# Attention scores of an encoder layer: from two 128-row products a head to three 64-row products a head, two heads in the two halves of the array

## Chip, cores and metric

The kernel runs on one core of one Trainium2 chip. The metric is the device time of one execution in microseconds; the time before is the median of three runs. TensorE does the matrix products. The profile calls its products PE and its loads of the stationary operand PEld. VectorE is DVE, ScalarE is ACT, GpSimd is POOL, and SyncE, whose queue issues nearly all transfers here, is SP.

## The reference, cut to what matters

One layer: RMSNorm, one wide input projection, two token mixers beside each other (chunked band attention with 8 heads of 64, and an mLSTM with 4 heads of 128), gates, an output projection, a feed-forward network with squared ReLU, a final RMSNorm. 2048 tokens, 1024 features, float32. The change lies in the band attention:

```
def chunk_band_attention(q, k, v, rel_bias):        # q, k, v: (1, 2048, 8, 64)
    # chunks of 64 tokens; a chunk sees itself and the 8 chunks before it
    scores = einsum('bclhd,bckhd->bchlk', qc, kband) * (1 / sqrt(64))
    scores = scores + bias                          # per head, by clipped distance
    scores = where(valid, scores, -1e30)
    p = softmax(scores, axis=-1)
    out = einsum('bchlk,bckhd->bclhd', p, vband)
```

## The kernel before

**Products in float32 from split operands.** Every float32 operand of a large product is held as two parts, a high part rounded to the matrix format (fp32r) and a low part that is the rest. ACT writes the high part, DVE subtracts it. The large products then take three matrix products, high by high, high by low and low by high (`mm3`, L488 to L490).

**Blocks.** The 2048 tokens are four blocks of 512. Blocks 0 and 1 ("near") are projected with plain tiles in `dense`. Blocks 2 and 3 ("far") are projected, together with the feed-forward network, by schemes of seven products of quarter matrices (`quad`, `quad_tok`, `down`; the products of L571 and L599), and their q and k come back from HBM: `parts` stores a high and a low part of each pair of heads to `qfar` and `kfar`. The attention of blocks 2 and 3 runs beside `down` of the first half.

**The order of the work** is set by a planner written in the kernel (`Flow`). Each piece of work is a generator that yields what it needs: `("pe", ns)`, `("act", ns)`, `("dve", ns)`, `("sp", ns, latency)` for a time on an engine, `"get"` for buffers of a pool, `"wait"` for events. The planner keeps a clock for each engine and gives the engine to the thread that can start first; the large products (priority 5) fill what is left. The order so found is the order in which each engine's queue is written, and each engine then executes its queue in order.

**Pools that the attention uses.** `rpool` has 28 tiles of 128 x 2 x 512, `bias` 2 of 128 x 640, `sc` 4 pairs of a score tile (128 x 640) and its statistics (128 x 4), `temp` 6 of 128 x 516, `banks` the 8 PSUM banks of 128 x 512.

**The attention of one block, per head h of pair j = h / 2:**

- Layout. A head's k tile has the high part of k in rows 0 to 63 and the low part in rows 64 to 127; column part 0 holds the block before, part 1 its own block. A head's q tile has the high part of q in both halves of the rows (part 0), and the low part in both (part 1). So one product over 128 rows adds q_high by k_high and q_high by k_low, and a second one adds q_low by both parts of k.
- Near blocks: `evac_q` (L1094) takes a bank of the projection, in which rows 0 to 63 are one head and rows 64 to 127 the other, and for each head writes the high part twice on ACT (L1101, L1103), the low part on DVE (L1105), and copies it on DVE (L1108). `evac_k` (L1113) writes high on ACT (L1120) and low on DVE (L1122). `spill_k` (L1128) stores k for the next block, and `head` (L1133) loads that of the block before.
- Far blocks: `head_far` (L1037) loads both parts of k and q of the head from HBM, q twice, for the two halves of the rows.
- `head_rest` (L1141) gets one bias tile, loads the head's bias (L1147), blocks out two corners on POOL (L1149, L1150), and starts two `unit`s, each for two query tiles of 128 tokens. The bias tile goes back at the end of both units.
- `unit` (L1170) gets two `sc` and starts `scores` for each of its tiles; when both are soft, it starts `turn` for groups of up to four 128 x 128 transposes (L1286, split by L1289 on ACT and L1291 on DVE), and `weigh`, the product with v (L1220).
- `scores` (L1244): a tile has 640 columns of keys (fewer in block 0), in two halves if it has over 256. Each half is two products (L1255) into a bank; DVE adds the bias and finds the extreme (L1261); then the exponential with its sum on ACT (L1270), the reciprocal (L1272) and the scaling on DVE (L1274).
- The end of `weigh`: v's two parts give two halves of the bank's rows; ACT copies one half (L1230), DVE adds the other (L1232), and the head's 64 rows are split into the mixer tile `mix[j]` by ACT (L1237) and DVE (L1239).

A block's scores go in groups of four products (two halves, two products each). A far block's attention has product groups of the scores, of the transposes and of `weigh` between products of `mm3`.

A place outside the attention that the prediction reads: `gates` (L1310) multiplies over 40 rows, so its stationary operand and its moving one lie in rows 0 to 39. It runs four times, once a block.

Of the kernel before, what the change touches and what calls it, by code (L numbers as in the profile page):

```python
# [29 lines left out]
P = 128  # L30
# [185 lines left out]
def dve_ns(n):  # L216
    return 70 + 1.042 * n
# [7 lines left out]
class Layer:  # L225
# [8 lines left out]
    def make_tiles(self, pool, psum):  # L234
# [36 lines left out]
        self.rec_room = Pool([0] * N_REC)  # L271
# [702 lines left out]
    def attention(self, b):  # L974
# [8 lines left out]
        for j in range(4):  # L983
# [9 lines left out]
            for i in range(2):  # L993
                h = 2 * j + i
                k, q = yield "get", self.rpool, 2
                B["kq"][h] = (k, q)
                fl.set(B["kq_ev"][h])
                fl.spawn(self.head(b, h), 1)
# [7 lines left out]
    def attention_far(self, b):  # L1006
# [7 lines left out]
        for j in range(4):  # L1014
# [12 lines left out]
            for i in range(2):  # L1027
                h = 2 * j + i
                k, q = yield "get", self.rpool, 2
                B["kq"][h] = (k, q)  # L1030
                fl.spawn(self.head_far(b, h), 1)
# [4 lines left out]
    def head_far(self, b, h):  # L1036
        fl, nc, B = self.fl, self.nc, self.blk[b]  # L1037
        k, q = B["kq"][h]
        j, rows = h // 2, slice(h % 2 * 64, h % 2 * 64 + 64)
        kf = k.bitcast(F32)  # L1040
        for n, x in ((0, b - 1), (1, b)):
            if x < 2:
                yield "wait", [self.blk[x]["k_spilt"][h]]
                yield "sp", 900, 2000
                nc.sync.dma_start(kf[:, n], self.kdram[x].ap().bitcast(F32)[h])
            else:
                yield "wait", [self.k_ev[x, j]]
                yield "sp", 900, 2000
                for a in range(2):
                    nc.sync.dma_start(kf[a * 64:a * 64 + 64, n], self.kfar[x].ap()[j, a, rows])  # L1050
        yield "wait", [self.q_ev[b, j]]
        yield "sp", 900, 2000
        for a in range(2):
            nc.sync.dma_start(q.bitcast(F32)[a * 64:a * 64 + 64],
                              self.qfar[b].ap()[j, :, rows].rearrange("a p c -> p a c"))
        fl.set(B["q_ev"][h])
        fl.set(B["k_ev"][h])
        yield from self.head_rest(b, h, k, q)
# [35 lines left out]
    def evac_q(self, b, j, bk):  # L1094
        fl, nc, B = self.fl, self.nc, self.blk[b]
        yield "wait", [B["kq_ev"][2 * j], B["kq_ev"][2 * j + 1]]
        for i in range(2):
            q = B["kq"][2 * j + i][1]
            src = bk[i * 64:i * 64 + 64]
            yield "act", act_ns(512, True)  # L1100
            nc.scalar.mul(q[0:64, 0], src, 0.125)  # L1101
            yield "act", act_ns(512, True)
            nc.scalar.mul(q[64:128, 0], src, 0.125)  # L1103
            yield "dve", dve_ns(512)
            nc.vector.scalar_tensor_tensor(q[0:64, 1], src, 0.125, q[0:64, 0].bitcast(F32),  # L1105
                                           op0=ALU.mult, op1=ALU.subtract)
            yield "dve", dve2_ns(512)
            nc.vector.tensor_copy(q[64:128, 1], q[0:64, 1].bitcast(F32))  # L1108
            fl.set(B["q_ev"][2 * j + i])
        fl.put_dense(self.banks, bk)  # L1110

    def evac_k(self, b, j, bk):
        fl, nc, B = self.fl, self.nc, self.blk[b]  # L1113
        yield "wait", [B["kq_ev"][2 * j], B["kq_ev"][2 * j + 1]]
        for i in range(2):
            h = 2 * j + i
            k = B["kq"][h][0]
            src = bk[i * 64:i * 64 + 64]
            yield "act", act_ns(512, True)
            nc.scalar.copy(k[0:64, 1], src)  # L1120
            yield "dve", dve_ns(512)
            nc.vector.tensor_sub(k[64:128, 1], src, k[0:64, 1].bitcast(F32))  # L1122
            fl.set(B["k_ev"][h])
            if b + 1 < NB:
                fl.spawn(self.spill_k(b, h, k), 2)
        fl.put_dense(self.banks, bk)

    def spill_k(self, b, h, k):  # L1128
        yield "sp", 900, 2000
        self.nc.sync.dma_start(self.kdram[b].ap().bitcast(F32)[h], k[:, 1].bitcast(F32))  # L1130
        self.fl.set(self.blk[b]["k_spilt"][h])

    def head(self, b, h):  # L1133
        fl, nc, B = self.fl, self.nc, self.blk[b]
        k, q = B["kq"][h]
        if b > 0:
            yield "wait", [self.blk[b - 1]["k_spilt"][h]]
            yield "sp", 900, 2000
            nc.sync.dma_start(k[:, 0].bitcast(F32), self.kdram[b - 1].ap().bitcast(F32)[h])
        yield from self.head_rest(b, h, k, q)  # L1140

    def head_rest(self, b, h, k, q):
        fl, nc, B = self.fl, self.nc, self.blk[b]
        (bias,) = yield "get", self.bias, 1
        yield "sp", 1500, 2000
        rb = self.io["rb"]
        nc.sync.dma_start(bias, bass.AP(rb.tensor, h * 768, [[1, P], [1, 640]]))  # L1147
        yield "pool", 180
        nc.gpsimd.memset(bias[0:64, 0:64], NEG)  # L1149
        nc.gpsimd.memset(bias[64:128, 576:640], NEG)  # L1150
        yield "wait", [B["q_ev"][h], B["k_ev"][h]]
# [1306 lines left out]
```

## Time and profile before

| | before |
|---|---|
| time, median of 3 runs | 2865.05 us (2863.65 to 2865.47) |
| profiled execution: span, first to last instruction | 2865.0 us |
| mean granted TensorE clock | 0.994 |
| PE busy | 2815.4 us, 98% |
| PEld busy | 2350.6 us, 82% |
| DVE busy | 2037.9 us, 71% |
| ACT busy | 1558.1 us, 54% |
| moved to and from HBM | 605.74 MB in packets, mean 211 GB/s |

The profiled execution's own time is its span, 2865.0 us; it lies between the lowest and the highest of the runs.

How to read it: "busy" is the union of an engine's instruction times. Products are pipelined, so the duration given for one product is longer than the time that it adds to a stream; the distance between the starts of two neighbours shows that. A group's row gives the line, the engine, the operation, the tiles and their shapes, the count, the busy time and the mean of one, then the idle time of the engine in front of these instructions and what ended it. In a timeline row the first number is the start and the second the length of the merged stretch, both in us. For matrix products "128*40" is rows by columns of the stationary operand.

### The profile page before, as it was taken

What the parts mean: (1) busy time and instruction counts of PE and PEld (TensorE: products, weight loads), DVE (VectorE), ACT (ScalarE), POOL (GpSimd) and SP (SyncE); (2) the same over time, 40 slices, a digit from 0 to 9 for tenths busy, and PEclk for the clock granted to TensorE, in tenths of its full rate; (3) what the DMA queues carried; (4) which work ended last, traced back from release to release, by engine and by line L of the source; (5) the groups of instructions that cost most, each with busy time, mean ns of one, the idle gap of its engine ahead of it and who ended that gap; (6) DMA issues with size and microseconds to landing.
All of it is one profiled execution on the core that took longest, in us unless ns stands there. A gap on an engine that the chain in (4) does not pass through costs nothing.

```text
span 2865.0 us, 39043 instructions
## 1 busy us (share of the span) xinstructions
PE 2815.4 (98%) x13576; PEld 2350.6 (82%) x13576; DVE 2037.9 (71%) x3783; ACT 1558.1 (54%) x2701; POOL 48.2 (2%) x116
## 2 busy tenths in 40 slices
PE   8999999999999999999999999999999999999998
PEld 7888888888878888877888888788778788888887
DVE  6886479778896867875666887778876744455565
ACT  4664366755444545664556666446644655554444
POOL 0000000000000000000000000000000000000000
PEclk9999999999999999999999999999999999999999
DMA  6327632357765768587878866577567655566563
GB/s 216 100 90 257 240 112 89 129 191 251 255 214 188 250 224 286 179 276 254 305 274 284 256 190 224 185 235 236 188 216 268 216 199 194 189 242 210 188 225 134
DMA packets 276005, 605.74 MB, mean 211 GB/s; under 512 B 30688, under 2 KB 45152, under 8 KB 275808
## 3 DMA queue, kind: packets, MB, share of 16 engines
q1 hardware_dynamic: 275808, 603.26, 62.6%
q8 instruction: 106, 1.74, 0.2%
q14 instruction: 91, 0.75, 0.1%
HBM read 426.98 MB, written 176.16 MB: 211 GB/s over the span
## 4 chain that ended last, share of the span: by engine, by line
PE 83%; DVE 7%; DMA 4%; ACT 3%; issue 1%; POOL 0%; SPq 0%; POOLq 0%; DVEq 0%; ACTq 0%
PE bank L571 36%; PE bank L488 12%; PE bank L489 12%; PE bank L490 12%; PE bank L599 2%; PE bank L1220 2%; PE bank L1255 2%; DMA r<-u 2%; PE bank L1286 1%; DVE wsp L429 1%; DVE r L968 1%; ACT wsp L427 1%; DVE sc L1261 1%; DVE r L1291 1%; DMA x<-ctx 1%
## 5 line engine op out<-in xcount | busy, mean ns | idle before, releaser
L571 PE MATMUL bank<-r,wsp 128*128 128x512 f32 x5208 | 1194.4, 391 | 9.4 <-DVE ctx L1772 7.2
L571 PEld LDWEIGHTS bank<-r,wsp 128*128 128x128 f32 x5208 | 980.0, 189 | 216.5 <-DVE ctx L1772 8.9
L429 DVE TENSOR_TENSOR wsp<-wraw,wsp 128x1024 fp32r<-128x1024 f32 x461 | 563.1, 1222 | 341.5 <-ACT wsp L427 299.0
L427 ACT CAST wsp<-wraw 128x1024 fp32r<-128x1024 f32 x461 | 484.2, 1051 | 493.7 <-PE bank L571 191.6
L488 PE MATMUL bank<-r,wsp 128*128 128x512 f32 x1600 | 640.7, 401 | 0.4 <-DVE ctx L1658 0.3
L490 PE MATMUL bank<-r,wsp 128*128 128x512 f32 x1600 | 625.2, 391 | 0.0
L489 PE MATMUL bank<-r,wsp 128*128 128x512 f32 x1600 | 624.8, 391 | 0.0
L490 PEld LDWEIGHTS bank<-r,wsp 128*128 128x128 f32 x1600 | 300.3, 188 | 64.6
L488 PEld LDWEIGHTS bank<-r,wsp 128*128 128x128 f32 x1600 | 301.1, 188 | 52.4 <-DVE ctx L1658 0.5
L489 PEld LDWEIGHTS bank<-r,wsp 128*128 128x128 f32 x1600 | 301.4, 188 | 51.7 <-DVE r L968 0.2
L1772 DVE TENSOR_TENSOR ctx<-bank,ctx 128x512 f32<-128x512 f32 x174 | 119.0, 687 | 85.2 <-PE bank L571 83.8
L963 ACT CAST r<-r 128x512 fp32r<-128x512 f32 x224 | 136.5, 622 | 78.0 <-DMA r<-u 74.2
L968 DVE TENSOR_TENSOR r<-r 128x512 fp32r<-128x512 f32 x224 | 149.7, 686 | 32.9 <-ACT r L963 31.8
L1270 ACT ACTIVATE sc<-sc,scs 128x640 f32<-128x640 f32 (+4 forms) x128 | 97.4, 761 | 77.1 <-DVE scs L1267 74.7
L1764 ACT COPY ctx<-bank 128x512 f32<-128x512 f32 x174 | 101.1, 582 | 66.7 <-PE bank L571 59.2
L396 DVE TENSOR_TENSOR ctx<-ctx,ctx 128x512 f32<-128x512 f32 x112 | 76.7, 688 | 73.5 <-DMA ctx<-in_wf 56.2
L2131 ACT ACTIVATE ctx<-ctx 128x512 f32<-128x512 f32 x96 | 60.6, 631 | 106.1 <-DVE ctx L1772 106.0
L1261 DVE CUSTOM_DVE_ANT_0 sc<-bank,bias 128x320 f32<-128x320 f32 (+3 forms) x240 | 104.6, 459 | 19.3 <-PE bank L1255 15.6
L1220 PE MATMUL bank<-r,r 128*128 128x256 f32 (+1 forms) x672 | 112.8, 288 | 5.6 <-DVE r L1291 3.6
L1220 PEld LDWEIGHTS bank<-r,r 128*128 128x128 f32 x672 | 100.4, 194 | 19.7 <-DVE r L1291 9.3
L1291 DVE TENSOR_TENSOR r<-bank,r 128x512 fp32r<-128x512 f32 (+1 forms) x168 | 96.9, 594 | 10.7 <-ACT r L1289 9.8
L1289 ACT CAST r<-bank 128x512 fp32r<-128x512 f32 (+1 forms) x168 | 81.8, 516 | 17.4 <-PE bank L1286 13.1
(275 smaller groups left out, 2884.9 us busy)
## 6 DMA issues: line engine op xcount, KB each, us to landing
wraw<-in_wf SPq DMA_DIRECT2D x170, 512.0 KB, 4.2
wraw<-wsum SPq DMA_DIRECT2D x136, 512.0 KB, 3.9
r<-u SPq DMA_DIRECT2D x224, 256.0 KB, 3.8
wraw<-in_w SPq DMA_DIRECT2D x104, 512.0 KB, 3.8
u<-ctx SPq DMA_DIRECT2D x128, 256.0 KB, 2.5
ctx<-in_wf SPq DMA_DIRECT2D x112, 256.0 KB, 4.3
wsum<-ctx SPq DMA_DIRECT2D x112, 256.0 KB, 3.6
u<-tmp SPq DMA_DIRECT2D x96, 256.0 KB, 2.9
```

Source lines behind the costliest of these rows:

```text
L427: nc.scalar.copy(w[:, 0], raw)
L429: nc.vector.tensor_sub(w[:, 1], raw, w[:, 0].bitcast(F32))
L488: mm(ps, lh, rh, start=first, stop=False)
L489: mm(ps, lh, rl, start=False, stop=False)
L490: mm(ps, ll, rh, start=False, stop=last)
L571: mm(ps, wv[:, x, k, n], a[:, y], start=new and k == 0 and x == y == 0, stop=k == 3 and x == 1, skip_group_check=True)
L963: self.nc.scalar.copy(dst[:, 0], src)
L968: self.nc.vector.tensor_sub(dst[:, 1], src, dst[:, 0].bitcast(F32))
L1220: nc.tensor.matmul(bk[:, c0:c0 + w], st, sl[:, x, o:o + w], start=n == 0, stop=n == total - 1)
L1261: nc.vector.tensor_tensor_reduce(out=e[:, x * w:x * w + w], in0=bks[x][:, :w], in1=br[:, j0 + x * w:j0 + x * w + w], op0=ALU.add, op1=ALU. ...
L1291: nc.vector.tensor_sub(slot[:, 1, :o], bk[:, :o], slot[:, 0, :o].bitcast(F32))
L1772: nc.vector.tensor_add(t[:, o:o + 512], ps, t[:, o:o + 512])
```

## The change

Two heads are handled as one pair. A pair has three `rpool` tiles: kh with the high part of k of both heads (one head in rows 0 to 63, the other in rows 64 to 127), kl with the low part, and q with the high part in column part 0 and the low part in part 1, again both heads in the two halves of the rows. For each stretch of columns six products are written, in the order (high, high), (low, high), (high, low) of q and k, and in each step first the upper half of the rows and then the lower, into two banks. A product then contracts 64 rows. The product of the low parts is left out, as `mm3` leaves it out.

With that: `evac_q` and `evac_k` write 128 rows in one instruction each on ACT and DVE; `pair_far` loads q and k of two heads at once; both bias tiles are taken and loaded for the pair and go back when all its scores are reduced; a `unit` is two query tiles of both heads, takes its score tiles two and two under a lock (`lane`), waits for the scores of both tiles, then turns and weighs one head after the other; the softmax is a thread of its own (`soften`); the split into the mixer tile waits for both heads and covers 128 rows (`join`). The planner is told 480 ns of PE for six products of one stretch, where it was told 500 for the four of a whole tile. The diff, cut to this:

```diff
     def evac_q(self, b, j, bk):
...
-        for i in range(2):
-            q = B["kq"][2 * j + i][1]
-            src = bk[i * 64:i * 64 + 64]
-            yield "act", act_ns(512, True)
-            nc.scalar.mul(q[0:64, 0], src, 0.125)
-            yield "act", act_ns(512, True)
-            nc.scalar.mul(q[64:128, 0], src, 0.125)
-            yield "dve", dve_ns(512)
-            nc.vector.scalar_tensor_tensor(q[0:64, 1], src, 0.125, q[0:64, 0].bitcast(F32),
-                                           op0=ALU.mult, op1=ALU.subtract)
-            yield "dve", dve2_ns(512)
-            nc.vector.tensor_copy(q[64:128, 1], q[0:64, 1].bitcast(F32))
+        q = B["kq"][j][2]
+        yield "act", act_ns(512, True)
+        nc.scalar.mul(q[:, 0], bk, 0.125)
+        yield "dve", dve_ns(512)
+        nc.vector.scalar_tensor_tensor(q[:, 1], bk, 0.125, q[:, 0].bitcast(F32), op0=ALU.mult, op1=ALU.subtract)
...
+    def pair_rest(self, b, j, k, q):
+        fl, nc, B = self.fl, self.nc, self.blk[b]
+        bias = yield "get", self.bias, 2
...
+        scored, done = [Event(), Event()], [Event(), Event()]
+        for u in range(2):
+            fl.spawn(self.unit(b, j, u, k, q, bias, scored[u], done[u]), 1)
+        yield "wait", scored
+        fl.put(self.bias, *bias)
...
+    def unit(self, b, j, u, k, q, bias, scored, done):
+
         fl, nc, B = self.fl, self.nc, self.blk[b]
+        yield "get", self.lane, 1
+        i0 = 2 * u
+        sct, evs, soft = {}, [Event(), Event()], [[Event(), Event()] for _ in range(2)]
+        for n in range(2):
+            sct[i0 + n] = yield "get", self.sc, 2
+            fl.spawn(self.scores(b, i0 + n, k, q, bias, sct[i0 + n], evs[n], [soft[a][n] for a in range(2)]), 1)
+        fl.put(self.lane, 0)
...
         yield "wait", evs
+        fl.set(scored)
+        (tmp,) = yield "get", self.temp, 1
+        ready = [Event(), Event()]
+        fl.spawn(self.join(b, j, u, tmp, ready, done), 1)
+        for a in range(2):
+            yield "wait", soft[a]
+            prob = {i: sct[i][a] for i in sct}
+            pev = [Event() for _ in pieces]
+            slots = [None] * len(pieces)
+            for n, pc in enumerate(pieces):
+                (slots[n],) = yield "get", B["pt"], 1
+                fl.spawn(self.turn(pc, slots[n], prob, first, pev[n]), 1)
+            fl.spawn(self.weigh(b, 2 * j + a, u, pieces, slots, pev, tmp, ready[a]), 1)
+            yield "wait", pev
+            fl.put(self.sc, *prob.values())
...
-        bks = yield "get", self.banks, halves
-        yield "pe", 500
-        for x in range(halves):
-            for y in range(2):
-                nc.tensor.matmul(bks[x][:, :w], q[:, y, i * P:(i + 1) * P],
-                                 kf[:, f * P + x * w:f * P + x * w + w], start=y == 0, stop=y == 1)
...
         for x in range(halves):
...
+            bks = yield "get", self.banks, 2
+            yield "pe", 480
+            c = f * P + x * w
+            for m, (y, z) in enumerate(((0, 0), (1, 0), (0, 1))):
+                for a in range(2):
+                    rows = slice(a * 64, a * 64 + 64)
+                    nc.tensor.matmul(bks[a][:, :w], q[rows, y, i * P:(i + 1) * P], kf[z][rows, c:c + w],
+                                     start=m == 0, stop=m == 2)
+            for a in range(2):
+                yield "dve", dve_ns(w)
+                e, st = scts[a]
+                nc.vector.tensor_tensor_reduce(
+                    out=e[:, x * w:x * w + w], in0=bks[a][:, :w], in1=bias[a][:, ::-1][:, j0 + x * w:j0 + x * w + w],
+                    op0=ALU.add, op1=ALU.min, scale=-1.0, scalar=3e38, accum_out=st[:, x:x + 1])
+                fl.put(self.banks, bks[a])
+                if x == halves - 1:
+                    fl.spawn(self.soften(scts[a], n, halves, soft[a]), 1)
+        fl.set(ev)
```

More of the change, by code (lines that the diff above doesn't have):

```diff
@@ L1169, in unit @@
[L1169 to L1180 removed]
+        yield "wait", [B["kq_ev"][j]]
+        kh, kl = B["kq"][j][:2]
@@ L1181, in unit @@
         cols = []
         for kt in range(min(first.values()), i0 + 6):
[L1183 removed]
+            use = [i for i in sct if first[i] <= kt <= i + 4]
             cols.append((kt, use))
```

217 lines of the change are left out of this document (87 added, 130 removed).

## The prediction

> **What bounds the kernel now.** I read the page from the top: busy times first, then the chain that ended last.
>
> ```profile
> PE 2815.4 (98%) x13576; PEld 2350.6 (82%) x13576; DVE 2037.9 (71%) x3783; ACT 1558.1 (54%) x2701; POOL 48.2 (2%) x116
> ...
> PE 83%; DVE 7%; DMA 4%; ACT 3%; issue 1%; POOL 0%; SPq 0%; POOLq 0%; DVEq 0%; ACTq 0%
> ```
>
> PE is busy for 2815 of 2865 us and is 83% of the chain, so nearly every microsecond given to or taken from PE's queue moves the end, and work taken from DVE or ACT moves it only where PE waits for them. The profiled execution spans 2865.0 us, the median of the three runs is 2865.05, so the sum is made against 2865.0 and needs no correction. What the scores cost stands in the groups by shape, first PE's, then the weight loads':
>
> ```profile
> L1255 PE MATMUL bank<-r,r 128*128 128x320 f32 x384 | 72.3, 312 | 1.3 <-DVE tmp L1232 0.8 <-DVE r L1122 0.5
> ...
> L1255 PE MATMUL bank<-r,r 128*128 128x256 f32 x48 | 8.9, 295 | 0.0
> ...
> L1255 PE MATMUL bank<-r,r 128*128 128x192 f32 x32 | 4.9, 274 | 0.0
> ...
> L1255 PE MATMUL bank<-r,r 128*128 128x128 f32 x16 | 3.1, 274 | 0.0
> ```
>
> ```profile
> L1255 PEld LDWEIGHTS bank<-r,r 128*128 128x128 f32 x480 | 73.7, 189 | 7.6 <-DVE tmp L1232 1.3 <-DVE r L1122 0.7
> ```
>
> The mean duration of one (312 ns) is a latency; products overlap. What one costs in a stream is the distance between starts, which the timeline of PE shows in a far block:
>
> ```profile
> 1642.18 0.39 PE L489 MATMUL bank<-r,wsp 128*128 128x512 f32 x1
> 1642.40 0.39 PE L490 MATMUL bank<-r,wsp 128*128 128x512 f32 x1
> 1642.64 1.25 PE L1286 MATMUL bank<-const,sc 128*128 128x128 f32 x10
> 1643.65 0.48 PE L488 MATMUL bank<-r,wsp 128*128 128x512 f32 x1
> 1643.96 0.39 PE L489 MATMUL bank<-r,wsp 128*128 128x512 f32 x1
> ...
> 1646.48 0.64 PE L1220 MATMUL bank<-r,r 128*128 128x256 f32 x4
> 1646.95 0.40 PE L488 MATMUL bank<-r,wsp 128*128 128x512 f32 x1
> ...
> 1647.65 0.75 PE L1255 MATMUL bank<-r,r 128*128 128x320 f32 x4
> 1648.23 0.64 PE L1220 MATMUL bank<-r,r 128*128 128x256 f32 x4
> ```
>
> So a product of 512 columns costs 0.23 us (1642.18 to 1642.40; over five of them, further down, 0.228), one of 320 costs 0.58 / 4 = 0.145, one of 256 0.47 / 4 = 0.118. One of 128 costs 0.11: from 1642.40 to 1643.96 are 1.56 us, less two products of 512 (0.46) leaves 1.10 for ten. The last is not 128 / 512 of 0.228 but the load: a weight load of 128 columns can start every 0.11 us. I use 0.11 for 192 columns too. The scores before are then 384 x 0.145 + 48 x 0.118 + 48 x 0.11 = 55.7 + 5.7 + 5.3 = **66.7 us** of PE.
>
> **The change part by part.**
>
> *Products.* Two heads and one stretch of columns took four products of 128 rows; they now take six of 64 rows, three for the upper half of the array and three for the lower, in turn. The number of products goes from 480 to 720. No row of this trace has two products in different halves at once, so I bound it. Best: the halves overlap fully, loads and products both, and six cost what three cost: 66.7 x 3/4 = 50.0, a gain of 16.7 us. Worst: nothing overlaps, 66.7 x 6/4 = 100.1, a loss of 33.4. Between them: the products overlap, but the loads follow one another at 0.11 as they do in every row here; then each of the 720 costs 0.11, 79.2 us, a loss of 12.5. I take the full overlap, because the two halves share no rows, no operand and no bank, and because loads and products of different instructions overlap already in the rows above; the other two are rivals.
>
> The Trainium skill, "TensorEngine Tiling (Array Packing)", Theoretical Speedup, gives a contraction of at most 64 rows up to 2x. By that alone the six would cost three, as in the best case; no run here shows it yet.
>
> *Change of rows.* This is the term against the change. The trace has few products of fewer rows within a stream of 128-row products; the plainest are those of the gates (L1310), on 40 rows. PE's timeline and that of the loads:
>
> ```profile
> 342.39 0.39 PE L488 MATMUL bank<-wsp,r 128*128 128x512 f32 x1
> ...
> 343.53 0.39 PE L490 MATMUL bank<-wsp,r 128*128 128x512 f32 x1
> 343.85 1.05 PE L1310 MATMUL bank<-sel,tmp 40*128 40x8 f32 x8
> 344.83 0.50 PE L488 MATMUL bank<-wsp,r 128*128 128x512 f32 x1
> 345.17 0.39 PE L489 MATMUL bank<-wsp,r 128*128 128x512 f32 x1
> ```
>
> ```profile
> 343.84 0.96 PEld L1310 LDWEIGHTS bank<-sel,tmp 40*128 40x128 f32 x8 [0.35 <-issue]
> 344.83 0.19 PEld L488 LDWEIGHTS bank<-wsp,r 128*128 128x128 f32 x1
> 344.94 0.19 PEld L489 LDWEIGHTS bank<-wsp,r 128*128 128x128 f32 x1
> 345.17 0.19 PEld L490 LDWEIGHTS bank<-wsp,r 128*128 128x128 f32 x1
> ```
>
> and, from the view of that one line, over the whole span:
>
> ```profile
> L1310 PEld LDWEIGHTS bank<-sel,tmp x32: 183/188/188, 39.5 to 851.3; 40*128 40x128 f32 x32
> ...
>   issue: 1.4, 4
> ```
>
> The five products from 342.39 to 343.53 give 0.228 for one. In a plain stream the next load starts with the product before it (345.17 and 345.17). Here the load of L1310 waits until 343.84, 0.31 after its predecessor's start: until the 0.228 of that product are over and 0.08 to 0.09 more, a drain. The load of the first 128-row product behind it waits again, to 344.83. "issue" says that nothing shown held it, and it is so in all four groups (0.35 of idle load path each), two in the near blocks, two in the far projections. From 343.53 to 345.17 are 1.64 us; two products of 512 and eight loads would take 0.46 + 0.88 = 1.34, and the ten transposes above, on 128 rows, fit that kind of sum. So one excursion costs 0.30 us here. For products of 320 columns I work it out from the parts: going in, the drain of 0.09 and the bare load of 0.11 are exposed, 0.20; coming out the same again, 0.20, since such a product is longer than a load, where the 8 columns of L1310 partly hid under one. That is **0.40 us a run** of scores, with 0.30 as the lower end. Behind the load that waits stands PE's whole stream.
>
> How many runs: in the changed program's order on PE the 720 products stand in 107 unbroken runs (88 of six, 12 of twelve, 7 others); before, the scores stood in 103. So 107 x 0.40 = 42.8 us, at the lower end 107 x 0.30 = 32.1.
>
> The same page of the Trainium skill, Key Properties, says that changing the tiling mode, not just the tile, drains the engine. The trace agrees on the mode (0.30 us at L1310); that going from the upper to the lower half inside a run is free stands on the rule alone. By the rule there are 107 drains out and back; without its distinction there would be one at nearly every product, which is the last rival below.
>
> *Copies.* The rows that shrink, ACT's and then DVE's:
>
> ```profile
> L1237 ACT CAST r<-tmp 64x256 fp32r<-64x256 f32 x64 | 25.8, 403 | 22.9 <-DVE tmp L1232 22.3
> ...
> L1103 ACT ACTIVATE r<-bank 64x512 fp32r<-64x512 f32 x16 | 9.5, 593 | 0.2
> L1101 ACT ACTIVATE r<-bank 64x512 fp32r<-64x512 f32 x16 | 9.5, 592 | 4.0 <-DVE r L1105 3.8
> ...
> L1120 ACT CAST r<-bank 64x512 fp32r<-64x512 f32 x16 | 9.3, 581 | 8.4 <-DVE r L1122 8.3
> ```
>
> ```profile
> L1239 DVE TENSOR_TENSOR r<-tmp,r 64x256 fp32r<-64x256 f32 x64 | 26.7, 417 | 3.9 <-ACT r L1237 2.7
> ...
> L1122 DVE TENSOR_TENSOR r<-bank,r 64x512 fp32r<-64x512 f32 x16 | 11.0, 690 | 2.3 <-ACT r L1120 1.8
> ...
> L1105 DVE SCALAR_TENSOR_TENSOR r<-bank,r 64x512 fp32r<-64x512 f32 x16 | 11.0, 687 | 4.3 <-ACT r L1103 4.0
> ...
> L1108 DVE CAST r<-r 64x512 fp32r<-64x512 f32 x16 | 6.7, 421 | 0.5
> ```
>
> An instruction on 128 partitions costs what one on 64 does:
>
> ```profile
> L968 DVE TENSOR_TENSOR r<-r 128x512 fp32r<-128x512 f32 x224 | 149.7, 686 | 32.9 <-ACT r L963 31.8
> ```
>
> So ACT goes from 54.1 us to 8 x 0.59 + 8 x 0.58 + 32 x 0.40 = 22.2, and DVE from 55.4 to 16 x 0.69 + 32 x 0.42 = 24.5. Thirty microseconds each, but on engines at 54% and 71%. The longest of PE's waits between 1565 and 2072 us, the far blocks' attention, is for softened tiles:
>
> ```profile
> PE bank L1286 <- DVE sc L1274: 6.4, 3, 2.9
> ```
>
> Of the saved DVE time only half of L1239's 13 us falls there, so I value the copies at 0 to -4 us.
>
> *Order and pools.* A unit now softens four tiles of two heads before the first transpose of either may go, where it was two tiles of one. Where PE has other work (both near blocks: gate products) this costs nothing; at the ends of the two far blocks it has less, and the 6.4 us above are waits of this kind. One tile costs DVE:
>
> ```profile
> L1261 DVE CUSTOM_DVE_ANT_0 sc<-bank,bias 128x320 f32<-128x320 f32 x192 | 87.7, 482 | 19.2 <-PE bank L1255 15.6 <-issue 2.6 <-POOL bias L1150 0.7
> ...
> L1274 DVE TENSOR_SCALAR sc<-sc,scs 128x640 f32<-128x640 f32 x96 | 52.8, 551 | 1.1
> ```
>
> 2 x 0.48 + 0.55 = 1.5 us, so two more are 3.0 at each of two ends: 0 to +6. Against the copies I book the two together at 0, bounds -4 and +6. Both bias tiles of a pair now load together; their issue waits on SP for the scores of the pair before, with weight loads queued behind it, and that pair's transposes and weighing hide it (before, it waited longer, for the head's end). By the code, the far blocks' loads of q go from 32 of 256 KB to 8 of 512, those of k from 48 of 128 KB to 24 of 256 where they come from the projections, and spilt k keeps its bytes. DVE's waits in the row of L1261 above end at PE for 15.6 us and at the bias tile's memset, behind its load, for 0.7, so I book 0; if that cover failed, the 0.7 would grow.
>
> *Sum.* 2865.0 - 16.7 + 42.8 + 0 = 2891.1, **2891 us**. With 0.30 a run and -4: 2876; with +6: 2897.
>
> **The rivals.**
>
> 1. *Loads in a line.* The products overlap, the loads do not, 0.11 each. +12.5 + 42.8: **2920 us** (2906 to 2926). For it: every load in the trace keeps 0.11 to its neighbour, that of 40 rows too. Against: they all go to the same rows.
> 2. *Nothing overlaps.* +33.4 + 42.8: **2941 us**.
> 3. *Faster: the rows of L1310 do not carry over.* If the pause is that instruction's own (8 columns, its operand), 64-row halves enter and leave the stream like any product, and the gain stands alone: 2865 - 16.7 = **2848 us**. It decides at 16.7 / 107 = 0.156 us a run: below that the change pays. For it: one kind of instruction is thin evidence. Against: all four groups show it, and "issue" says that the operand was there.
> 4. *The drain is partly hidden*, about 0.16 a run, by queues that would have stalled PE anyway: **2865 us** (2858 to 2872).
> 5. *Every change of half drains.* Some 600 changes inside the runs at 0.20: over **2960 us**.
>
> **How the numbers follow.** The forecast 0.48, loads in a line 0.26, nothing overlaps 0.06, no drain 0.11, partly hidden 0.06, every half drains 0.03. The likeliest gives 2891, its own range 2876 to 2897. The range takes the forecast, rival 1 and rival 4: 2860 to 2926, with 0.80 in it. A measurement here tells 0.2% (6 us) from no change. Faster: rival 3 and a sixth of rival 4, 0.12. Same: half of rival 4, 0.03. Slower: the rest, 0.85.
>
> **What would show it.** In the profile after, the loads of the scores start about 0.3 us after their predecessor's start at each run's beginning, with "issue" as the reason, and so does the next 128-row load: right; if they follow at 0, rival 3. Inside a run of six products of 320 columns, the starts come in pairs, and the pairs 0.145 apart: right; single starts at 0.11, rival 1; at 0.145, rival 2. PE's busy share stays near 98% and DVE's total falls by some 30 us. A PE wait on DVE at the far blocks' ends that is more than 6 us longer, or a span moved while the runs of scores are as short as before, would make the prediction wrong in a way that I have not priced.

## The result, and the profile after

| | before | after |
|---|---|---|
| median of 4 runs each | 2865.26 us (2863.65 to 2868.89) | 2913.73 us (2910.17 to 2918.06) |
| ratio, 95% interval | | 1.0166 (1.0151 to 1.0180) |
| profiled execution: span | 2865.0 us | 2909.8 us |
| mean granted TensorE clock | 0.994 | 0.991 |

The change makes the kernel slower, by 1.5 to 1.8%: 48.5 us by the medians, 44.8 by the two profiled spans. The forecast was +26, its own range 2876 to 2897 us. Busy times and the chain that ended last, from the page of after:

```profile
PE 2848.1 (98%) x13816; PEld 2343.3 (81%) x13816; DVE 2015.0 (69%) x3719; ACT 1523.6 (52%) x2637; POOL 51.8 (2%) x116
...
PE 67%; DVE 6%; DMA 4%; issue 2%; ACT 1%; POOL 0%; SPq 0%; POOLq 0%; DVEq 0%; ACTq 0%
```

PE is still at 98%, and it still sets the end: the chain could be followed back to 576 us only, its shares add up to 80%, and of these PE has 67, as it had 83 of 98 before. PE's 32.7 us more of busy time are no measure of the loss: the row does not say that a product ran in a stream with its neighbours or was waiting at half clock. The scores by shape, PE's groups and then the weight loads':

```profile
L1247 PE MATMUL bank<-r,r 64*128 64x320 f32 x576 | 70.2, 339 | 1.4 <-DVE tmp L1227 1.0 <-ACT ctx L1569 0.2
...
L1247 PE MATMUL bank<-r,r 64*128 64x256 f32 x72 | 7.1, 303 | 0.0
```

```profile
L1247 PEld LDWEIGHTS bank<-r,r 64*128 64x128 f32 x720 | 55.1, 185 | 29.9 <-issue 15.7 <-DVE scs L1252 2.2 <-DVE tmp L1227 2.0
```

576 products of 64 rows keep PE as long as 384 of 128 rows did (70.2 against 72.3 us), and 720 loads take less of the load path than 480 did (55.1 against 73.7): two of them run at once. The new thing is the idle time in front of the loads: 29.9 us where it was 7.6, and half of it (15.7) ended by "issue". PE's timeline around one run of six in a far block, then that of the loads:

```profile
1687.86 0.39 PE L489 MATMUL bank<-r,wsp 128*128 128x512 f32 x1
1688.09 0.39 PE L490 MATMUL bank<-r,wsp 128*128 128x512 f32 x1
1688.40 0.71 PE L1247 MATMUL bank<-r,r 64*128 64x320 f32 x6
1689.04 0.50 PE L488 MATMUL bank<-r,wsp 128*128 128x512 f32 x1
1689.37 0.39 PE L489 MATMUL bank<-r,wsp 128*128 128x512 f32 x1
```

```profile
1687.86 0.19 PEld L490 LDWEIGHTS bank<-r,wsp 128*128 128x128 f32 x1
1688.40 0.44 PEld L1247 LDWEIGHTS bank<-r,r 64*128 64x128 f32 x6 [0.35 <-issue]
1689.04 0.19 PEld L488 LDWEIGHTS bank<-r,wsp 128*128 128x128 f32 x1 [0.19 <-issue]
1689.15 0.19 PEld L489 LDWEIGHTS bank<-r,wsp 128*128 128x128 f32 x1
```

The load of L490 starts with the product before it (1687.86 and 1687.86). The first load of the scores starts 0.31 after the start of L490's product, and the first load behind the run waits again. From the start of L490 to that of L489 are 1.28 us; two products of 512 columns and three steps of 0.145 would take 0.46 + 0.435 = 0.90. The run costs **0.39 us** beyond its products. Inside it, the single records start in pairs 3 to 4 ns apart, loads too, and the pairs stand 0.143 to 0.145 apart, but for 0.248 from the first to the second, which holds a bare load.

**Where the 44.8 us lie.** I compared, in the two traces, the starts of the n-th large product (those of 512 columns in L571, L488 to L490 and L599, which come in the same number in both). When the near blocks' attention is done in both, the changed kernel has lost 11.8 us, ahead of the far blocks' attention 10.4, behind it 44.8, and it stays there. So the near blocks cost 11.8 and the far blocks 34.4. By the prediction's own terms the near blocks owe 48 x 0.40 - 7.3 = 11.9, and the far ones 59 x 0.40 - 9.3 = 14.3. What was not foreseen, some 20 us, lies in the far blocks alone, and the windows show where: the columns are the stretch, the busy times of PE, PEld, DVE, ACT and POOL with their counts, the granted clock, the DMA share and GB/s. After:

```profile
1980.00:2040.00 60.00, 59.99 (x323) 48.66 (x322) 46.71 (x106) 36.77 (x73) 0.58 (x4) 1.00 0.63 212
2040.00:2100.00 60.00, 46.24 (x268) 38.48 (x267) 41.18 (x128) 33.52 (x84) 3.88 (x9) 0.77 0.37 117
2100.00:2145.00 45.00, 40.07 (x216) 33.18 (x215) 29.42 (x73) 18.34 (x45) 1.01 (x1) 0.96 0.47 148
```

The same stretches of before:

```profile
1980.00:2040.00 60.00, 58.88 (x341) 50.84 (x340) 52.97 (x125) 37.46 (x84) 1.13 (x2) 1.00 0.52 168
2040.00:2100.00 60.00, 54.15 (x284) 45.15 (x283) 41.29 (x89) 30.55 (x67) 3.52 (x4) 0.94 0.66 221
2100.00:2145.00 45.00, 45.00 (x201) 37.12 (x201) 38.25 (x55) 22.86 (x34) 0.00 (x0) 1.00 0.67 227
```

Most of the GB/s are the weights of the large products. After, they flow early (212 against 168 before 2040) and are missing later (117 against 221, then 148 against 227): the large products have run ahead, and the attention that they should have stood beside is left over. It begins late, too: the first run of far scores starts at 1600.41 us, at 1567.03 before. PE is idle for 13.8 us of the 60 behind 2040 (60 - 46.24), and its clock falls to 0.77. What PE does there, and what it waits for, in the timeline of after and in PE's three longest waits between 2040 and 2130:

```profile
2059.71 1.27 PE L1247 MATMUL bank<-r,r 64*128 64x320 f32 x9
2062.00 2.89 PE L1247 MATMUL bank<-r,r 64*128 64x320 f32 x15 [1.02 <-DVE tmp L1227]
...
2085.30 0.71 PE L1247 MATMUL bank<-r,r 64*128 64x320 f32 x6
2091.24 0.69 PE L1631 MATMUL bank<-const,ctx 128*128 128x128 f32 x2 [5.23 <-DVE ctx L1620]
```

```profile
PE bank L1631 <- DVE ctx L1620: 6.3, 2, 5.2
PE bank L1284 <- DVE sc L1272: 2.3, 2, 1.8
PE bank L2274 <- DVE r L1289: 1.9, 1, 1.9
```

Scores, transposes and the recurrence stand alone there, each at the mercy of DVE and ACT: a run of scores waits until DVE is through with the sum at the end of a weighing (L1227), and the 5.2 us at L1631 are the end of the other mixer, small steps on DVE and POOL one after the other, for which PE waits 0.3 us in the same stretch of before (its L1633).

The same two large products bound the whole stretch of the far blocks' attention. Before, then after:

```profile
1550.56:2300.06 749.50, 728.49 (x3787) 616.96 (x3785) 583.42 (x1277) 426.98 (x826) 16.46 (x44) 0.99 0.69 221
```

```profile
1560.94:2344.85 783.91, 751.88 (x3914) 615.89 (x3913) 578.91 (x1261) 419.42 (x810) 15.99 (x44) 0.98 0.63 206
```

PE is idle for 21.0 us of it before (749.50 - 728.49) and for 32.0 after, 11.0 more. The trace's clock records grant half the clock for 20.5 us of it before and for 37.5 after; half of the 17.0 more, 8.5 us, is an estimate of what that costs PE (ten transposes take 2.56 us at 2068.59, within such a stretch, and 1.25 in the prediction's timeline), and an upper one, since it was idle in a part of it. With the 14.3 owed that makes 33.8 of the 34.4.

### The profile page after: what moved, and what is told of

Its sections match the earlier page's. It is cut to its first block, busy times and chain, and to the rows that moved or that the text cites. A ratio compares the mean times of both kernels' runs of the same rounds, so it can differ in the third digit from the quotient of the medians.

```text
span 2909.8 us, 39351 instructions
## 1 busy us (share of the span) xinstructions
PE 2848.1 (98%) x13816; PEld 2343.3 (81%) x13816; DVE 2015.0 (69%) x3719; ACT 1523.6 (52%) x2637; POOL 51.8 (2%) x116
## 4 chain that ended last, share of the span: by engine, by line
PE 67%; DVE 6%; DMA 4%; issue 2%; ACT 1%; POOL 0%; SPq 0%; POOLq 0%; DVEq 0%; ACTq 0%
PE bank L571 34%; PE bank L488 8%; PE bank L489 8%; PE bank L490 8%; PE bank L599 2%; PE bank L1216 1%; PE bank L1247 1%; DVE wsp L429 1%; DMA r<-u 1%; PE bank L1284 1%; DMA ctx<-in_wf 1%; DVE r L970 1%; DMA ctx<-x 0%; DVE r L968 0%; DMA ctx<-yp 0%
## 5 line engine op out<-in xcount | busy, mean ns | idle before, releaser
L571 PE MATMUL bank<-r,wsp 128*128 128x512 f32 x5208 | 1190.0, 390 | 8.3 <-DVE ctx L1770 5.5
L571 PEld LDWEIGHTS bank<-r,wsp 128*128 128x128 f32 x5208 | 976.8, 188 | 214.5 <-DVE ctx L1770 7.2
L488 PE MATMUL bank<-r,wsp 128*128 128x512 f32 x1600 | 645.6, 404 | 0.0
L490 PE MATMUL bank<-r,wsp 128*128 128x512 f32 x1600 | 625.7, 391 | 0.0
L489 PE MATMUL bank<-r,wsp 128*128 128x512 f32 x1600 | 625.3, 391 | 0.0
L488 PEld LDWEIGHTS bank<-r,wsp 128*128 128x128 f32 x1600 | 301.6, 188 | 64.7 <-issue 9.2
L490 PEld LDWEIGHTS bank<-r,wsp 128*128 128x128 f32 x1600 | 300.9, 188 | 65.1 <-issue 0.2
L489 PEld LDWEIGHTS bank<-r,wsp 128*128 128x128 f32 x1600 | 301.9, 189 | 53.1
```

The lines of the kernel that those rows point to most:

```text
L488: mm(ps, lh, rh, start=first, stop=False)
L489: mm(ps, lh, rl, start=False, stop=False)
L490: mm(ps, ll, rh, start=False, stop=last)
L571: mm(ps, wv[:, x, k, n], a[:, y], start=new and k == 0 and x == y == 0, stop=k == 3 and x == 1, skip_group_check=True)
```

## The experiments

"Near" is the loss against before up to the end of the near blocks' attention, "far" the loss across that of the far blocks, both by the starts of the large products (after: +11.8 and +34.4). The changed kernel profiled again (experiment 12) has +9.4 and +38.5, and experiment 5, whose queue has the same order of groups, +9.2 and +31.8; so a difference of 3 us near or 7 us far between two traces says nothing. All are edits of the changed kernel, except 2 and 3, which are edits of the kernel before.

**1. The change's order without its products.** Four products of 128 rows again, in the changed program's groups (each adds up the rows of both heads, so the scores are not the heads' own):

```diff
-            for m, (y, z) in enumerate(((0, 0), (1, 0), (0, 1))):
-                for a in range(2):
-                    rows = slice(a * 64, a * 64 + 64)
-                    nc.tensor.matmul(bks[a][:, :w], q[rows, y, i * P:(i + 1) * P], kf[z][rows, c:c + w],
-                                     start=m == 0, stop=m == 2)
+            for a in range(2):
+                for y in range(2):
+                    nc.tensor.matmul(bks[a][:, :w], q[:, y, i * P:(i + 1) * P], kf[0][:, c:c + w],
+                                     start=y == 0, stop=y == 1)
```

> The changed program and its order, but each group of six products of 64 rows is four products of 128 rows (each adds up both heads' rows, so the scores are not the heads' own): no change of rows, no overlap of halves. Theory: the 107 runs pay 0.40 us each for going in and out of 64 rows (42.8) and gain 16.7 by the overlap, so this is 26 us below the changed kernel's 2914: about 2888, and the 22 us that remain above before's 2865 are the order of the far blocks' attention. Rival: the change of rows is the whole loss of 48 and the order costs nothing: 2865. Rival: the change of rows costs nothing and the order is all: 2914 + 17 = 2930.

Measured: 2882.93 us (2874.75 to 2886.90), ratio 1.0057 (1.0036 to 1.0079); span 2885.1; near +0.8, far +18.2. Order, pools and copies by themselves cost some 18 us (10 to 23 by the interval), nearly all of it in the far blocks; the near blocks get them for nothing. The stretch that was thin in after is thin here too:

```profile
2040.00:2100.00 60.00, 45.33 (x263) 39.20 (x263) 44.18 (x145) 34.85 (x96) 3.17 (x6) 0.83 0.22 63
```

What is left for the 64-row products is 2909.8 - 2885.1 = 24.7 by the spans and 26 to 31 by the ratios (1.0149 or 1.0166, the two comparisons of after, less 1.0057), where the prediction had 42.8 - 16.7 = 26.1.

**2 and 3. The price of one excursion, in the kernel before.** Behind each of its 128 groups of scores one more product of 8 columns, on 64 rows in the first kernel and on 128 in the second; nothing reads its columns:

```diff
+        nc.tensor.matmul(bks[0][:, 504:512], q[0:64, 0, i * P:(i + 1) * P], kf[0:64, f * P:f * P + 8],
+                         start=True, stop=True)
```

```diff
+        nc.tensor.matmul(bks[0][:, 504:512], q[:, 0, i * P:(i + 1) * P], kf[:, f * P:f * P + 8],
+                         start=True, stop=True)
```

> The kernel before, with one product of 64 rows and 8 columns added behind each of its 128 groups of score products, into columns of the bank that nobody reads. Theory (each excursion into 64 rows drains PE going in and coming out): 128 x (0.30 + 0.11) = 52 us, 2917. Rival (no drain, the product costs its load alone): 128 x 0.11 = 14 us, 2879.

> The control to the small product of 64 rows: the kernel before with one product of 128 rows and 8 columns behind each of the 128 groups. Theory: it costs its load, 128 x 0.11 = 14 us at most, 2873 to 2879, so that of the 37 us of the 64-row one some 25 are the change of rows. Rival (any added product breaks the stream and costs about the same): 2897 to 2902.

Measured: 64 rows 2902.09 us (2898.99 to 2903.69), ratio 1.0129 (1.0108 to 1.0149); 128 rows 2876.01 (2871.46 to 2880.59), ratio 1.0043 (1.0029 to 1.0056). A product of 8 columns on the same rows costs 12 to 13 us, 0.10 each, which is its load. On 64 rows it costs three times that. The timeline of the 64-row kernel:

```profile
1659.67 0.39 PE L490 MATMUL bank<-r,wsp 128*128 128x512 f32 x1
1659.90 0.74 PE L1255 MATMUL bank<-r,r 128*128 128x320 f32 x4
1660.57 0.27 PE L1257 MATMUL bank<-r,r 64*128 64x8 f32 x1
1660.77 0.49 PE L488 MATMUL bank<-r,wsp 128*128 128x512 f32 x1
1661.10 0.39 PE L489 MATMUL bank<-r,wsp 128*128 128x512 f32 x1
```

From 1659.90 to 1661.10 are 1.20 us; four steps of 0.145 and one of 0.23 make 0.81. The excursion costs 0.39 in the stream with its own product, 0.29 more than the product on 128 rows. Over the whole, 52 were expected and 37 came: near +21.7 of 26, far +12 of 26. In the far blocks about half of the pauses fell where PE would have waited anyway: over the stretch bounded as above, its idle time falls from 21.0 us to 13.1 (761.35 - 748.23); the prediction's rival 4 is right about this part of the kernel, and about nothing else.

**4. Do the two halves overlap because they are two halves?** Both heads of a group multiply in the upper rows (the second head's scores are then those of the first):

```diff
-                    rows = slice(a * 64, a * 64 + 64)
+                    rows = slice(0, 64)
```

> The changed kernel, but both heads' products use rows 0 to 63 (the second head's scores are those of the first): 720 products of 64 rows, none in the lower half. Theory (the overlap is of the two halves): six slots of 0.145 in place of three, 50 us of PE more, 2950 to 2964 with what the far blocks' waits take up. Rival (64-row products overlap in whatever half): 2914.

Measured: 2946.29 us (2941.24 to 2951.79), ratio 1.0284 (1.0264 to 1.0304); near +30.9 instead of +11.8.

```profile
467.39 0.39 PE L490 MATMUL bank<-r,wsp 128*128 128x512 f32 x1
467.71 1.14 PE L1247 MATMUL bank<-r,r 64*128 64x320 f32 x6
468.78 0.39 PE L1216 MATMUL bank<-r,r 128*128 128x256 f32 x1
```

The six now take 1.07 us (467.71 to 468.78) where after's took 0.64 (1688.40 to 1689.04): the difference of 0.43 is three steps of 0.145. The overlap belongs to the two halves.

**5. Must the halves take turns?** All three products of the upper half first, then the three of the lower:

```diff
-            for m, (y, z) in enumerate(((0, 0), (1, 0), (0, 1))):
-                for a in range(2):
-                    rows = slice(a * 64, a * 64 + 64)
+            for a in range(2):
+                rows = slice(a * 64, a * 64 + 64)
+                for m, (y, z) in enumerate(((0, 0), (1, 0), (0, 1))):
```

> The changed kernel with the six products of a group in another order: the three of the upper half first, then the three of the lower; same products, same banks. Theory (products enter in order and overlap only with a neighbour in the other half): five slots of 0.145 instead of three, 120 groups x 0.29 = 35 us more, 2935 to 2949 with what the far blocks' waits take up. Rival (the array runs the two halves' queues apart, whatever the order): 2914. Rival (no overlap at all in this order): six slots, 2950 to 2966.

Measured: 2904.40 us (2902.79 to 2906.93), ratio 1.0146 (1.0129 to 1.0163). My theory, that neighbours in the queue have to be of different halves, falls. The run takes what it took:

```profile
1686.12 0.39 PE L490 MATMUL bank<-r,wsp 128*128 128x512 f32 x1
1686.43 0.71 PE L1247 MATMUL bank<-r,r 64*128 64x320 f32 x6
1687.08 0.50 PE L488 MATMUL bank<-r,wsp 128*128 128x512 f32 x1
1687.41 0.39 PE L489 MATMUL bank<-r,wsp 128*128 128x512 f32 x1
```

From L490 to L489 are 1.29 us, 1.28 in after. In the single records the six start in three pairs, 5 to 11 ns apart. Two products have to signal a finished bank, the third and the sixth as written; in 64 of the 88 runs of six, the records that carry a signal are the last pair and no other. So the fourth, as written, does not wait for the second and the third.

**6. Twice as many products in a run, in the near blocks.** Both stretches of a tile in one group, four banks, in blocks 0 and 1 (87 runs instead of 107):

```diff
-        for x in range(halves):
-            bks = yield "get", self.banks, 2
-            yield "pe", 480
...
+        xs = list(range(halves))
+        for part in ([xs] if b < 2 else [[x] for x in xs]):
+            bks = yield "get", self.banks, 2 * len(part)
+            yield "pe", 480 * len(part)
+            for o, x in enumerate(part):
...
+                        nc.tensor.matmul(bks[2 * o + a][:, :w], q[rows, y, i * P:(i + 1) * P], kf[z][rows, c:c + w],
+                                         start=m == 0, stop=m == 2)
```

> The changed kernel, but in blocks 0 and 1 both stretches of a tile are written as one group of twelve products into four banks: 87 runs of scores instead of 107, the same products. Theory (a run pays 0.40 us whatever its length): 20 x 0.40 = 8 us less, 2906, and blocks 0 and 1 together lose about 3 us on the kernel before instead of 10.8 by the profile's starts of the large products. Rival (the cost goes with the number of products, not of runs): 2914 and 10.8 as before.

Measured: 2907.09 us (2903.27 to 2908.61), ratio 1.0153 (1.0136 to 1.0170); near +4.7. With after's +11.8 and, again, +9.4, 20 runs fewer give 4.7 to 7.1 us, 0.24 to 0.36 a run, where 8 were expected. The same near blocks in 9 and 10 stand at +12.9 and +6.6. Fewer runs are cheaper in each pairing, but the traces lie too far apart for a price. The timeline of a run of twelve gives it:

```profile
387.04 0.39 PE L490 MATMUL bank<-r,wsp 128*128 128x512 f32 x1
387.36 1.15 PE L1249 MATMUL bank<-r,r 64*128 64x320 f32 x12
388.44 0.50 PE L488 MATMUL bank<-r,wsp 128*128 128x512 f32 x1
388.77 0.40 PE L489 MATMUL bank<-r,wsp 128*128 128x512 f32 x1
```

From L490 to L489 are 1.73 us; two products of 512 columns and six steps of 0.145 make 1.33. Twelve products pay 0.40 as six do: the cost goes with the runs, not with the products. By the whole time, against after's two comparisons of 1.0166 and 1.0149, nothing can be said.

**7. Fewer waits for bias tiles.** Pairs 1 and 3 take over the bias tiles of pairs 0 and 2, without loading their own (their scores get the wrong heads' bias):

```diff
-        bias = yield "get", self.bias, 2
+        first = j % 2 == 0
+        if first:
+            B["bias_ev", j // 2] = Event()
+            B["bias", j // 2] = yield "get", self.bias, 2
+        else:
+            yield "wait", [B["bias_ev", j // 2]]
+        bias = B["bias", j // 2]
...
-        for i in range(2):
+        for i in range(2 if first else 0):
...
-        fl.put(self.bias, *bias)
+        B["scored", j // 2] = B.get(("scored", j // 2), 0) + 1
+        if B["scored", j // 2] == 2:
+            fl.put(self.bias, *bias)
```

> The changed kernel, but the two bias tiles loaded for pair 0 serve pair 1 too, and those of pair 2 serve pair 3 (the bias of every second pair is left out). Theory: with two bias tiles, a pair's scores wait in the planner's order until the pair before has all its scores and the new tiles have landed; this pushes the far blocks' attention behind the large products, and 15 to 20 us of it run with nothing beside them. Without every second wait: 2895 to 2900. Rival: the far blocks are late because a unit holds all four score tiles until its four softmaxes are done; then nothing changes: 2911 to 2916.

Measured: 2902.13 us (2895.72 to 2905.53), ratio 1.0128 (1.0103 to 1.0152); far +20.8 instead of +34.4. By the stage the gate counts: two of four of them are worth some 14 us in the far blocks (11 to 18 against the three traces of after's order). By the whole time it is less sure, since the interval overlaps with that of after's second comparison (1.0132 to 1.0166). The edit also takes half of the bias loads away; what their bytes are worth by themselves was not tried.

**8 and 9. Tell the planner what PE pays.** 840 ns for a group, the 0.435 + 0.40 that it takes, everywhere, and then in the far blocks alone:

```diff
-            yield "pe", 480
+            yield "pe", 840
```

```diff
-            yield "pe", 480
+            yield "pe", 480 if b < 2 else 840
```

> The changed kernel with one number changed: the planner is told 840 ns of PE for a group of six, about what a run costs (0.44 + 0.40), where it was told 480. Theory: the far excess is one of order, so an order that spreads attention over the large products takes some of the 20 us back: 2894 to 2905. Rival: the excess is in the work itself (drains, softmax of four tiles): 2911 to 2916.

> The changed kernel, with the planner told 840 ns a group in blocks 2 and 3 alone, 480 in blocks 0 and 1. With 840 everywhere the far part took some 14 us less and the near part some 4 to 9 more. Theory (the far excess is the order of the queue): the far part keeps its 14, the near part stays as in the changed kernel: 2898 to 2902. Rival (the gain was chance between runs): 2911 to 2916.

Measured: everywhere 2905.22 us (2899.63 to 2907.32), ratio 1.0135 (1.0109 to 1.0161), far +19.9, near worse (+15, and +20 ahead of the far blocks' attention); in the far blocks alone 2895.83 (2894.99 to 2896.31), ratio 1.0115 (1.0099 to 1.0131), near +12.9, far +19.5. Nothing is computed otherwise, only the order differs, and the far blocks get back 15 us. The thin stretch does not go away; PE gets more done in it, 287 products in place of 268, at a clock of 0.86:

```profile
2040.00:2100.00 60.00, 46.08 (x287) 37.30 (x285) 47.80 (x157) 37.12 (x100) 2.82 (x8) 0.86 0.41 125
```

**10. The best that I found of the change.** Runs of twelve in the near blocks (as in 6) and 840 in the far ones (as in 9), put together.

> The two corrections together: groups of twelve in blocks 0 and 1, the planner told 840 ns in blocks 2 and 3. Theory (runs and order add up): 8 less by the runs and 14 less by the order than the changed kernel, 2888 to 2894, ratio 1.008 to 1.010, still slower than before, since 85 runs x 0.40 = 34 are over the gain of 16.7. Rival (the order of the far blocks is chance and undoes it): 2900 to 2910.

Measured: 2895.59 us (2892.40 to 2899.32), ratio 1.0107 (1.0090 to 1.0124); near +6.6, far +21.7. It is no better than 9 within the intervals, a little slower than I expected, and still slower than the kernel before.

**11. Bias tiles kept (as in 7) and 840 in the far blocks (as in 9).**

> The planner told 840 ns in blocks 2 and 3, and the bias of every second pair left out, as in the earlier run. Theory (both act on the same waits of the far blocks' queue): little beyond the 840 alone, 2890 to 2896. Rival (they are two separate costs and add up): 2882 to 2886.

Measured: 2889.27 us (2887.53 to 2891.95), ratio 1.0085 (1.0070 to 1.0101); far +8.8. That is 25.6 less than after, nearly the sum of the two (13.6 + 14.9), and below the 14.3 that products and runs owe there: of the far blocks' excess nothing is left. My theory, that both act on the same waits and bring little together (2890 to 2896), is missed, and so is the rival's sum (2882 to 2886); the time lies between, the stage speaks for the sum. The same window as above:

```profile
2040.00:2100.00 60.00, 49.41 (x325) 40.72 (x325) 47.62 (x139) 38.56 (x100) 3.13 (x4) 0.94 0.40 133
```

The granted clock is back at before's 0.94, and PE issues 325 products there, 268 in after.

**12. After again,** unchanged, beside the later kernels:

> The changed kernel unchanged, beside the others of this call, to compare on one chip: ratio to the kernel before 1.015 to 1.018. If the group's order of the run with the upper half first matters, this is 1.0166 against its 1.0146; if chips and runs differ by that much, it comes nearer.

Measured: 2908.26 us (2906.51 to 2912.06) against 2866.39 for before, ratio 1.0149 (1.0132 to 1.0166). Two comparisons of one kernel thus differ by 0.0017, 5 us; smaller differences above rest on the stages, not on the medians.

**What the far blocks' loss is made of.** The sum made above for after, 14.3 us for products and runs (0 in experiment 1), what PE is idle beyond the 21.0 of before, and half of what it stands at half clock beyond the 20.5 of before, for the other traces, in us:

| | idle | at half clock | by the sum | far, measured |
|---|---|---|---|---|
| after | 32.0 | 37.5 | 33.8 | 34.4 |
| 12, after again | 31.8 | 47.8 | 38.7 | 38.5 |
| 1, products of 128 rows | 30.1 | 37.5 | 17.6 | 18.2 |
| 7, bias tiles kept | 27.4 | 17.1 | 18.9 | 20.8 |
| 9, 840 in the far blocks | 25.3 | 20.5 | 18.6 | 19.5 |
| 11, both | 19.8 | 10.2 | 8.0 | 8.8 |

So the excess of after is idle time and half clock in nearly equal parts, and the edits of the order take away both.

## Why the prediction was right, and where it fell short

- **Products: right.** Full overlap was forecast, 66.7 to 50.0 us. Runs of six take three steps of 0.145, loads go in pairs, and with both heads in one half the three steps come back (experiment 4). Rivals 1 and 2 fall, though rival 1's 2920 lies near the time measured: its mechanism, loads 0.11 apart, is not in the trace. The Trainium skill, "TensorEngine Tiling (Array Packing)", Theoretical Speedup, with its "up to 2x" for 64 rows, is borne out inside a run: 1.07 us against 0.64 with the pauses in both, 0.87 against 0.435 without.
- **Change of rows: right.** 0.40 us a run was forecast from products of 40 rows; 0.39 stands in after's timeline. The 8 columns of experiment 2 pay 0.29 beyond a load, as the 8 columns of L1310 paid 0.30, so it is right, too, that a short product hides a part. A run of twelve pays 0.40 (experiment 6). Rival 3, no pause, falls: the change decides at 0.156 us a run, and it is 0.40. Rival 5 falls, too: going from half to half is free, in turn or not. Rival 4 holds for extra pauses in the far blocks of before, by half. The two terms together, +26.1, measure 24.7 by the spans between experiment 1 and after, 26 to 31 by the ratios.
- **Copies: as forecast,** and worth nothing. The rows of DVE after, first the join, then the split of k and of q:

```profile
L1195 DVE TENSOR_TENSOR r<-tmp,r 128x256 fp32r<-128x256 f32 x32 | 13.4, 420 | 3.3 <-ACT r L1193 3.3
...
L1098 DVE TENSOR_TENSOR r<-bank,r 128x512 fp32r<-128x512 f32 x8 | 5.5, 687 | 0.1
L1087 DVE SCALAR_TENSOR_TENSOR r<-bank,r 128x512 fp32r<-128x512 f32 x8 | 5.5, 682 | 0.0
```

13.4 + 5.5 + 5.5 = 24.4 us, 24.5 forecast. DVE's total falls by 22.9, not by 30, and experiment 1 has them all for no gain in the near blocks.
- **Order and pools: the step that failed.** It was booked at 0 (-4 to +6, with the copies) and costs some 18 (experiment 1). The prediction's sentences were that two softened tiles more are "3.0 at each of two ends" and that the pair's "transposes and weighing hide" the bias loads. Both price a wait by its own length. The sign named for the bias loads, DVE's 0.7 us at the bias tile growing, does not appear: the row of after has no wait for a bias tile left.

```profile
L1252 DVE CUSTOM_DVE_ANT_0 sc<-bank,bias 128x320 f32<-128x320 f32 x192 | 87.0, 484 | 14.4 <-PE bank L1247 13.7
```

The planner had written the queue around it. What it costs is the order: while a pair waits in the planner for two bias tiles, and for all scores of the pair before, PE's queue is filled with large products, and these are then missing beside the attention that is left over, for some 80 us (2041 to 2120) in which each wait of DVE, ACT and of the recurrence is PE's own. "What would show it" had named a PE wait at the far blocks' ends more than 6 us longer as unpriced; PE's idle time there grew by 11.0, in many waits. The planner adds to it, since it was told 480 ns for what takes 840.
- **What is shown of this cause, and what is open.** Experiments 7 and 9 act on the bias gate and on the planner's price; each takes 14 to 15 us out of the far blocks, and both together (11) the whole excess. That the large products run ahead is not the whole story: their farthest lead over before, by the same starts, is 18.8 us in after, but 12.8 in 7, 11.7 in 11 and even 22.3 in 9, which loses 15 us less. How the attention that is left over is laid out counts as well, and how much was not taken apart. Nor is it shown how much of it the score tiles do, four held by a unit where there were two, and the first pair's larger loads of q, k and bias: more bias or score tiles were not tried. The lower clock behind 2040 (0.77) goes when the order is mended (0.94), so I count it to the price of the order, not as a cause of its own; it is up to 8.5 of the some 20 us.

The forecast of 2891 is what the change would cost had its order been free; of the 22.6 us that are missing some 18 are this one term, and the rest is no more than what the two comparisons of after differ by (5). That 2914 lies in the stated range of 2860 to 2926 is luck: the forecast's own range ended at 2897, and the upper end was set by rival 1, whose mechanism is not there.

## What to carry to other kernels

Count the excursions, not the products. Six products on two halves of 64 rows take three steps where four products of 128 rows took four, because the product of the low parts is left out; but each unbroken run of such products among 128-row ones costs 0.40 us here, so a run has to save more than that before it pays (six products in place of four saved 0.145, and twelve in place of eight 0.29). Make the runs long, or keep the whole stage on 64 rows. When a change pairs what was single, ask which resource now gates the next unit, and what the planner puts into PE's queue meanwhile; here the price was paid where that filler was missing later, in idle time and a lower clock, and not where the wait was.

## What the runs showed of the hardware

- Products of the two halves start out of the written order: with U U U L L L in the queue they run as three pairs (experiment 5). The Trainium skill, "TensorE: Matmul & The Clock Gate", The mechanism, has products start and end strictly in program order; experiment 5's records disagree with it for different halves: the run takes the time of three pairs, and the sixth product, known by its signal, starts 5 to 11 ns from the third.
- Loads of the two halves run at once, 182 to 186 ns each and 3 to 4 ns apart, where 128-row loads keep 0.11 to each other.
- The pause of a run of scores lies half before and half behind it, each a drain of 0.08 to 0.09 and a bare load of 0.11; one product of 8 columns on 64 rows takes 0.39 in all, while on 128 rows it costs its load alone (0.10).
